# Linear attention's last two heads spread over the values' products, with operands, weight pages and weight sums at other places

## The chip, the cores and the metric

The kernel runs on one core of a Trainium2 chip. The metric is the device time of one execution in microseconds. The kernel before takes 2302.86 us, the median of three runs (2300.2, 2302.86 and 2305.18).

## The reference

One layer of a streaming encoder, 512 frames of width 2048, all in float32. A normalised input goes through one projection whose columns feed banded softmax attention (16 heads of 64), and gated linear attention (4 heads, keys of 128, values of 256). Both results go through `w_out`, then a gated feed-forward block with a short convolution, then an embedding gate, then a last normalisation.

```python
h = rms_norm(x, norm_mix_w[i])
proj = h @ w_in[i]
q_a, k_a, v_a, q_g, k_g, v_g, r_g, gate_lr = split_cols(proj, IN_SPLITS)
y_a = chunked_band_attention(q_a, k_a, v_a, att_rel_bias[i])
o_g = gated_linear_attention(q_g, k_g, v_g, log_a)
y_g = rms_norm(o_g, gla_norm_w[i]) * jax.nn.silu(r_g)
x = x + concat([y_a, y_g]) @ w_out[i]
h = rms_norm(x, norm_ffn_w[i])
u = causal_depthwise_conv(h @ w_ffn_up[i], w_ffn_conv[i], b_ffn_conv[i])
x = x + (gelu(u_gate) * u_val) @ w_ffn_down[i]
h = rms_norm(x, norm_ple_w[i])
x = x + sigmoid(h @ w_ple_gate[i]) * (p[i] @ w_ple_proj[i])
return rms_norm(x, final_norm_w)
```

## The kernel before

Every weight travels as a **page** of 128 x 1024 float32 (512 KB). A page is loaded by a DMA that SyncE issues, ScalarE copies it to a rounded high part, VectorE subtracts to get the low part, and TensorE multiplies three times (high by high, high by low, low by high). `wtile` does this for one page. Raw pages, high parts and low parts come from three **rings** of three buffers each (`wr`, `wh`, `wl`), so the raw page n+3 can be loaded only after VectorE has split page n, and the high part n+3 can be written only after TensorE has done with page n.

Large products are done with seven block products instead of eight (`PLAIN`: P1, P2, P6, P5, P7, P3, P4). Each multiplies a block of the weights, or a sum of blocks, by a block of the activations, or a sum of blocks. The activations' seven **operands** (R11, R21, N2, N1, T3, R22, T4) lie in DRAM after the first stage; `Stage.load` brings one half of one operand back (512 KB), `Stage.split` makes its two parts. The weight sums S1 to S4 are made ahead in DRAM: `sum_begin` copies a block from DRAM to DRAM on SyncE's queue, `sum_add` adds a second block with an accumulating DMA on GpSimd's queue. A list of such steps (`sum_chores`) is worked off either by `wtile` (one step a page, from the list `chores`) or at numbered steps of the later stages (`agenda`).

The order of stages:

1. The values of linear attention, and its four heads. `gla_proj(hd)` makes the decays and the two projections `pk` and `pq`; `gla_core(hd)` is a generator in six pieces, run piece by piece: the decayed keys (`kd2`, `eb2`); the transposes `pkt`, the matrix `pat`, the copy `kT` and the masked `attnT`; the states `pu` and `S`; the outputs `po` and their squares; the norm `msw`, `rg`; the last scaling and the store to `ond`.
2. **The values' products** of softmax attention: 7 products of 4 pages, 28 pages in all, 12 matmuls a page into `va`. Pages are fetched two ahead (`value_fetch(v, n + 2)`). The last pieces of heads 2 and 3 of linear attention stand between the pages of P1 and P2 (`beside_first`, `beside_second`).
3. Two units of the embedding's product (`pp`), then the **front** stage: 8 units with the attention heads and 4 with the output gates. Then `w_out` (`wo`), the up projection (`up`), and the rest.

Each engine works in the order of its own queue. VectorE, ScalarE and TensorE instructions made while `in_order(True)` is set keep the program's order; elsewhere a list scheduler may move them. SyncE's and GpSimd's queues are also in order: a DMA that waits holds up all that stand behind it on its queue. A front unit takes raw pages from a list `free`; a page returns when it has been split (`used`), and `issue` then starts the next load that is `wanted`. A name with a star keeps one free page back for a sum that VectorE makes.

What the change touches: `wtile` (line 123), the list `free` (line 393), the sums' places in the agenda (line 960), `values_product` (line 1116), and the run of the last two heads and of the values' products (lines 1351 to 1415).

Of the kernel before, what the change touches and what calls it, by code (L numbers as in the profile page):

```python
# [8 lines left out]
F32 = mybir.dt.float32  # L9
F32R = mybir.dt.float32r  # L10
# [4 lines left out]
P = 128  # L15
# [17 lines left out]
PLAIN = ("P1", "P2", "P6", "P5", "P7", "P3", "P4")  # L33
# [9 lines left out]
def encoder_block(ctx: ExitStack, tc: tile.TileContext, A, out):  # L43
# [29 lines left out]
    def in_order(on):  # L73
        for e in (vec, act, ten):
            e.on = on
# [20 lines left out]
    def use_rings(new):  # L96
        rings.update(new)
        for ring in new:
            counts[ring] = 0
# [18 lines left out]
    def psum_aux(name):  # L118
        return aux[0](name)

    chores, hold = [], [True]

    def wtile(src, name, parts=1, between=None):
        n = src.shape[1]
        raw = page("wr", name + "_r")
        hi, lo = page("wh", name + "_h", F32R), page("wl", name + "_l", F32R)
        w = n // parts
        for i in range(parts):
            if i and between is not None:
                between()  # L130
            c = slice(i * w, (i + 1) * w)
            nc.sync.dma_start(raw[:, c], src[:, c])
            act.activation(hi[:, c], raw[:, c], AF.Copy)
            vec.tensor_tensor(lo[:, c], raw[:, c], hi[:, c].bitcast(F32), ALU.subtract)
        if chores and hold[0]:
            chores.pop(0)()
        return hi, lo

    def mm3(po, whi, wlo, act, start, stop):
# [136 lines left out]
    xa, xb = [], []  # L276
# [33 lines left out]
    X_TAGS = [(op, g) for op in PRODUCT_OPERANDS for g in range(2)]  # L310
# [79 lines left out]
            self.o = None  # L390
            self.banks = {}

    free = [f"r{i}" for i in (3, 4, 5)]
    wanted = []

    def raw_page(unit, name):
# [88 lines left out]
    def prep(i, own=None):  # L485
        prep_low(prep_high(i, own))
# [230 lines left out]
    ps_, early = [], []  # L717
# [187 lines left out]
    agenda = [[] for _ in range(len(steps) + 60)]  # L905
# [28 lines left out]
    def embedding_load(raw):  # L934
        nc.sync.dma_start(raw.rearrange("p (k t) -> p k t", k=2), A["p"].rearrange("k p t -> p k t"))
        return raw

    def embedding_split(raw, t):
        ps_[:] = [t.rearrange("p h (k t) -> p k h t", k=2)]
        act.activation(t[:, 0, :], raw, AF.Copy)  # L940
        vec.tensor_tensor(t[:, 1, :], raw, t[:, 0, :].bitcast(F32), ALU.subtract)

    raws = {}
# [13 lines left out]
        aux_tags[:] = ["b6", "b7"]  # L957
        banks.extend(("b4", "b5"))

    for i, f in enumerate(sum_chores(summed[:4])):  # L960
        agenda[2 + 5 * i + 3 * max(i - 10, 0)].append((0, f))
    for i, f in enumerate(sum_chores(summed[4:])):
        agenda[base[stages[4].units[2]] + 5 * i].append((0, f))
    agenda[base[front.units[7]] + 7 + 12].append((5, attention_done))
# [112 lines left out]
    def norm_root():  # L1077
        norm["w"] = rstd_begin(norm["ms"])

    value_sums = {}  # L1080

    def value_page(name, j):
        if name[0] == "S":
# [21 lines left out]
    def values_begin():  # L1105
        v = dict(ps=[psum_mm(f"va{i}") for i in range(4)], pages=[(p, j) for p in PLAIN for j in range(4)], tiles={}, have=set())
        for n in range(2):
            value_fetch(v, n)
        return v
# [3 lines left out]
            prod, j = v["pages"][n]  # L1113
            v["tiles"][n] = wtile(value_page(PRODUCTS[prod][0], j), f"wva_{prod}{j}")

    def values_product(v, prod, between=None):
        _, op, b = PRODUCTS[prod]
        acc2 = v["ps"][0:2] if b == "A" else v["ps"][2:4]
        fresh = prod in ("P1", "P2", "P5")
        for j in range(4):  # L1120
            n = 4 * PLAIN.index(prod) + j
            value_fetch(v, n + 2)
            if between is not None:
                between(j)
            hi, lo = v["tiles"].pop(n)
            for i in range(2):
                k = 2 * j + i
                x = front.x[op, k // 4]
                wh, wl = hi[:, i * T:(i + 1) * T], lo[:, i * T:(i + 1) * T]
                for t in range(2):  # L1130
                    sl = slice(k % 4 * 256 + t * P, k % 4 * 256 + t * P + P)
                    kw = {} if fresh else {"skip_group_check": True}
                    first, last = fresh and k == 0, k == 7
                    ten.matmul(acc2[t], x[:, 0, sl], wh, start=first, stop=False, **kw)
                    ten.matmul(acc2[t], x[:, 0, sl], wl, start=False, stop=False, **kw)
                    ten.matmul(acc2[t], x[:, 1, sl], wh, start=False, stop=last, **kw)

    def values_collect(v, prod):
        quarter, sign = {"P1": ("C11", 1), "P2": ("C11", 1), "P6": ("C12", 1), "P5": ("C22", -1),
                         "P7": ("C22", -1), "P3": ("C12", 1), "P4": ("C21", -1)}[prod]  # L1140
# [15 lines left out]
    with ExitStack() as mix:  # L1156
        vp = mix.enter_context(tc.tile_pool(name="v", bufs=1, side="right"))

        with ExitStack() as gctx:
            gp = gctx.enter_context(tc.tile_pool(name="gla", bufs=1, side="right"))  # L1160
            reset = gp.tile([P, T], F32, name="reset")
            nc.gpsimd.memset(reset, 1.0)
# [16 lines left out]
                store_pair(h1d, k, xslot(k, ""), xslot(k + 8, ""), gp.tile([P, 1024], F32, tag="tp", name="tp", bufs=2))  # L1179

            for c in range(2):
                hold[0] = c == 0
                vproj(A["w_v_g"], c, lambda t: V[:, t, c * T:(c + 1) * T], c == 0, input_pair if c else None)
            hold[0] = True

            upr = page("wr", "up_r")[:, :T]
            nc.gpsimd.memset(upr[96:P], 0.0)
# [163 lines left out]
            cores = [gla_core(2, *st)]  # L1351
            step = lambda n: next(cores[n], None)

            def middle():
                in_order(True)
                for n in range(2):
                    step(0)
                in_order(False)

            nxt = gla_proj(3, middle)  # L1360
            cores.append(gla_core(3, *nxt))
            hctx.close()
            xb.append(ctx.enter_context(tc.tile_pool(name="xb", bufs=1, reuse_waits="tile")))
            pad = xb[0].tile([P, 8], F32, tag="pad", name="pad")
            nc.gpsimd.memset(pad, 0.0)
            for op, g in X_TAGS[:8]:
                front.load(op, g)
            in_order(True)
            va = values_begin()
            for g in range(2):  # L1370
                front.split("R11", g)
            step(0)
            nxt[-1]()

            def beside_first(j):
                if j:
                    step(0)
                if j > 1:
                    front.split("R21", j - 2)
                    step(1)  # L1380

            def beside_second(j):
                step(1)
                if j % 2:
                    front.split("N2", j // 2)

            values_product(va, "P1", beside_first)
            values_collect(va, "P1")
            values_product(va, "P2", beside_second)
            values_collect(va, "P2")  # L1390

    xa.append(ctx.enter_context(tc.tile_pool(name="xa", bufs=1, side="right", reuse_waits="tile")))
    for op, g in X_TAGS[8:]:
        front.load(op, g)

    ectx = ExitStack()
    early.append(ectx.enter_context(tc.tile_pool(name="early", bufs=1, side="right", reuse_waits="tile")))
    raws["p"] = embedding_load(early[0].tile([P, 1024], F32, tag="pT", name="pT"))

    values_product(va, "P6", lambda j: front.split("N1", j // 2) if j % 2 else None)  # L1400
    values_collect(va, "P6")
    values_product(va, "P5", lambda j: front.split("T3", j // 2) if j % 2 else None)
    values_collect(va, "P5")
    values_product(va, "P7", lambda j: front.split("R22", j // 2) if j % 2 else None)
    embedding_split(raws["p"], early[0].tile([P, 2, 1024], F32R, tag="ps", name="ps"))
    values_collect(va, "P7")
    issue()
    values_product(va, "P3", lambda j: front.split("T4", j // 2) if j % 2 else None)
    values_collect(va, "P3")
    values_product(va, "P4")  # L1410
    free.extend(("r0", "r1", "r2"))
    issue()
    prep(0)
    prep(1)
    values_collect(va, "P4")
# [276 lines left out]
```

## Time and profile before

| what | us |
|---|---|
| median of three runs | 2302.86 |
| the profiled execution, its own time | 2303.16 |
| its span, first to last instruction | 2300.8 |
| VectorE busy | 1878.6 |
| ScalarE busy | 1312.1 |
| GpSimd busy | 183.8 |

The span is 2.4 us shorter than the time of the same execution. TensorE's granted clock is 0.99 of full speed over the whole span. A busy time is a sum over one engine. An idle time in square brackets in a timeline row is the idle time of that engine just before the instruction, with what ended it. A DMA share is the mean busy share of the core's 16 DMA engines in a stretch.

### The profile page before, as it was taken

Reading aid. Unit: us, or ns where it says so; the run is one execution under the profiler, and the core shown is the slowest. Engines: PE = TensorE matmul, PEld = TensorE weight load, DVE = VectorE, ACT = ScalarE, POOL = GpSimd, SP = SyncE. Lnnn points to the kernel's source line nnn. Section 1 sums busy time; section 2 is a strip of 40 time slices with the busy share of each in tenths; the row PEclk is TensorE's granted clock in tenths of the full one; section 3 lists DMA queues with packets and bytes.
Section 4 is the critical chain, followed back from the end, with each engine's and each line's share of the span. In section 5 each row is a group of like instructions: output and inputs, shape, how many; then the busy total and the mean of one; then the engine's idle time right before and its main releaser. Section 6 shows DMA issues by size and latency. Waiting matters only on the chain.

```text
span 2300.8 us, 45116 instructions
## 1 busy us (share of the span) xinstructions
PE 2252.0 (98%) x17960; PEld 2180.4 (95%) x17960; DVE 1878.6 (82%) x2580; ACT 1312.1 (57%) x1925; POOL 183.8 (8%) x225
## 2 busy tenths in 40 slices
PE   9998799999989999999999999999999999999997
PEld 7787679999989999999999999999999999999997
DVE  7556567988678888899888888888888787898987
ACT  6354456776565575555555555555564454656766
POOL 0010000110100001111111111000000000000000
PEclk9999999999999999999999999999999999999999
DMA  7985578888898898999999987777786876968896
GB/s 273 276 229 184 190 226 246 234 228 233 254 379 257 268 314 224 282 291 290 289 274 277 275 237 217 211 217 206 225 299 216 270 236 212 349 234 321 290 286 208
DMA packets 215219, 588.09 MB, mean 256 GB/s; under 512 B 23168, under 2 KB 74624, under 8 KB 215008
## 3 DMA queue, kind: packets, MB, share of 16 engines
q1 hardware_dynamic: 181568, 474.28, 57.8%
q0 software_dynamic: 29952, 107.49, 25.2%
q10 hardware_dynamic: 3488, 3.44, 0.4%
q8 instruction: 140, 2.29, 0.4%
q14 instruction: 71, 0.58, 0.1%
HBM read 506.48 MB, written 141.56 MB: 282 GB/s over the span
## 4 chain that ended last, share of the span: by engine, by line
PE 85%; DMA 5%; DVE 5%; ACT 2%; issue 1%; SPq 0%; DVEq 0%; ACTq 0%
PE accA L65 42%; PE accC L65 21%; PE accB L65 10%; PE va L65 2%; DVE wl L65 1%; PE pp L65 1%; PE psc L65 1%; DMA on<-ond 1%; DMA wv_r<-in_w_v_g 1%; PE ptr L65 1%; PE py L65 1%; PE v L264 1%; PE v L263 1%; PE v L265 1%; DMA wo_N<-mix_N 1%
## 5 line engine op out<-in xcount | busy, mean ns | idle before, releaser
L65 DVE TENSOR_TENSOR wl<-s,wh 128x1024 fp32r<-128x1024 f32 (+1 forms) x365 | 437.6, 1199 | 71.6 <-ACT wh L65 70.6
L65 ACT ACTIVATE wh<-l 128x1024 fp32r<-128x1024 f32 (+1 forms) x308 | 319.1, 1037 | 183.3 <-PE accC L65 118.1
L65 DVE TENSOR_TENSOR wl<-l,wh 128x1024 fp32r<-128x1024 f32 (+1 forms) x308 | 367.6, 1193 | 57.2 <-ACT wh L65 56.8
L65 ACT ACTIVATE wh<-s 128x1024 fp32r<-128x1024 f32 (+1 forms) x365 | 378.1, 1036 | 35.4 <-DVE s L65 21.0
L65 ACT ACTIVATE u<-accA 128x256 f32<-128x256 f32 x290 | 109.7, 378 | 366.2 <-PE accA L65 365.9
L65 DVE TENSOR_TENSOR s<-s,l 128x1024 f32<-128x1024 f32 (+1 forms) x168 | 201.4, 1199 | 9.9 <-DMA s<-in_w_blk 9.2
L65 PE MATMUL accA<-up_T,wh 128*128 128x256 f32 x1408 | 178.8, 279 | 0.0
L65 PEld LDWEIGHTS accA<-up_T,wh 128*128 128x128 f32 x1408 | 170.3, 188 | 0.0
L65 DVE SCALAR_TENSOR_TENSOR cv<-u,cw,cv 128x511 f32<-128x511 f32 (+1 forms) x176 | 131.6, 748 | 3.1
L426 POOL DMA_DIRECT2D s<-in_w_up x84 | 74.2, 883 | 733.0 <-DMA s<-in_w_up 366.5
L65 PE MATMUL accA<-up_T,wl 128*128 128x256 f32 x704 | 96.6, 279 | 0.0
L65 PE MATMUL accA<-dn_T,wh 128*128 128x256 f32 x704 | 90.1, 279 | 0.0
L65 PE MATMUL accA<-up_R,wh 128*128 128x256 f32 x704 | 89.8, 280 | 0.0
L65 DVE TENSOR_TENSOR u<-u,accC 128x256 f32<-128x256 f32 x98 | 40.9, 418 | 59.5 <-PE accC L65 58.3
L65 PE MATMUL accA<-up_N,wh 128*128 128x256 f32 x704 | 89.4, 279 | 0.0
L65 PE MATMUL accC<-up_N,wh 128*128 128x256 f32 x704 | 89.4, 279 | 0.0
L65 PE MATMUL accC<-up_R,wh 128*128 128x256 f32 x704 | 89.4, 279 | 0.0
L65 PE MATMUL accB<-up_R,wh 128*128 128x256 f32 x704 | 89.4, 279 | 0.0
L65 PEld LDWEIGHTS accA<-up_T,wl 128*128 128x128 f32 x704 | 88.1, 188 | 0.0
L65 ACT ACTIVATE u<-accC 128x256 f32<-128x256 f32 x94 | 36.0, 383 | 89.5 <-PE accC L65 88.8
L65 PEld LDWEIGHTS accA<-dn_T,wh 128*128 128x128 f32 x704 | 85.7, 188 | 0.0
L65 PEld LDWEIGHTS accA<-up_R,wh 128*128 128x128 f32 x704 | 85.2, 188 | 0.5 <-issue 0.5
(426 smaller groups left out, 5257.4 us busy)
## 6 DMA issues: line engine op xcount, KB each, us to landing
l<-in_w_up SPq DMA_DIRECT2D x132, 512.0 KB, 6.6
s<-in_w_up SPq DMA_DIRECT2D x84, 512.0 KB, 6.1
s<-in_w_up POOLq DMA_DIRECT2D x84, 512.0 KB, 7.6
l<-in_w_dn SPq DMA_DIRECT2D x56, 448.0 KB, 4.9
l<-in_w_blk SPq DMA_DIRECT2D x36, 512.0 KB, 5.7
l<-in_w_out SPq DMA_DIRECT2D x28, 512.0 KB, 5.5
l<-in_w_dn SPq DMA_DIRECT2D x28, 512.0 KB, 5.4
s<-in_w_blk SPq DMA_DIRECT2D x24, 512.0 KB, 5.2
```

Of the source, the lines that this page charges most:

```text
L65: ins = f(*args, **kw)
L263: nc.tensor.matmul(ps[t], h1[kt][:, 0, sl], wh, start=kt == 0, stop=False)
L264: nc.tensor.matmul(ps[t], h1[kt][:, 0, sl], wl, start=False, stop=False)
L265: nc.tensor.matmul(ps[t], h1[kt][:, 1, sl], wh, start=False, stop=kt == KD - 1)
L426: nc.gpsimd.dma_start(t, src("L22" if name == "S1" else "L11"), accum_op=ALU.add)
```

## The change

- `wtile` works off as many steps of `chores` as `hold[0]` says, instead of one or none.
- The sums of the first two `wo` units (4 copies and 4 adds each) leave the agenda of the front stage. They are put on `chores` ahead of head 3's projections, with two steps a page there and one a page afterwards. The sums of the first two `up` units stay in the agenda, now at steps 2, 9, 16 and so on to 65 instead of 42 to 108.
- The first piece of head 2's core is issued ahead of `gla_proj(3)`, and only the second piece in its middle.
- Head 3's pieces and head 2's last ones are set to fixed pages of the values' products by a table `plan`; head 3 stands one page further from head 2.
- The operands are loaded in the program two halves of an operand at a time, at set pages, instead of eight halves ahead of P1 and six behind P2. The splits are set to pages as well.
- The raw ring has six pages from the values' products on (r3, r4, r5, r2, r0, r1 instead of three). So r3 to r5 are no longer free for the front stage's first loads; all six come free at page 25, with `issue`.

```diff
-    chores, hold = [], [True]
+    chores, hold = [], [1]
...
-        if chores and hold[0]:
-            chores.pop(0)()
+        for _ in range(hold[0]):
+            if chores:
+                chores.pop(0)()
...
-    free = [f"r{i}" for i in (3, 4, 5)]
+    free = []
...
-    for i, f in enumerate(sum_chores(summed[:4])):
-        agenda[2 + 5 * i + 3 * max(i - 10, 0)].append((0, f))
+    for i, f in enumerate(sum_chores(summed[2:4])):
+        agenda[2 + 7 * i].append((0, f))
...
             value_fetch(v, n + 2)
-            if between is not None:
-                between(j)
+            for f in plan.get(n, ()):
+                f()
...
-            def middle():
+            def pinned(f):
                 in_order(True)
-                for n in range(2):
-                    step(0)
+                f()
                 in_order(False)
 
-            nxt = gla_proj(3, middle)
+            pinned(lambda: step(0))
+            chores.extend(sum_chores(summed[:2]))
+            hold[0] = 2
+            nxt = gla_proj(3, lambda: pinned(lambda: step(0)))
+            hold[0] = 1
...
-            for op, g in X_TAGS[:8]:
-                front.load(op, g)
-            in_order(True)
-            va = values_begin()
-            for g in range(2):
-                front.split("R11", g)
-            step(0)
-            nxt[-1]()
...
-            def beside_first(j):
-                if j:
-                    step(0)
-                if j > 1:
-                    front.split("R21", j - 2)
-                    step(1)
-
-            def beside_second(j):
-                step(1)
-                if j % 2:
-                    front.split("N2", j // 2)
...
-    for op, g in X_TAGS[8:]:
-        front.load(op, g)
...
-    values_product(va, "P4")
-    free.extend(("r0", "r1", "r2"))
-    issue()
...
+    for page_, k in ((1, 0), (3, 0), (4, 0), (2, 1), (4, 1), (5, 1), (6, 1), (8, 1), (9, 1)):
+        at_page(page_, lambda k=k: step(k))
+    at_page(10, gla_done)
+    at_page(16, open_early)
+    for op, loads, splits in (("R21", (0, 1), (2, 3)), ("N2", (2, 3), (5, 7)), ("N1", (4, 5), (9, 11)), ("T3", (10, 11), (13, 15)),
+                              ("R22", (12, 13), (17, 19)), ("T4", (14, 15), (21, 23))):
+        for g in range(2):
+            at_page(loads[g], lambda op=op, g=g: front.load(op, g))
+            at_page(splits[g], lambda op=op, g=g: front.split(op, g))
+    at_page(20, lambda: embedding_split(raws["p"], early[0].tile([P, 2, 1024], F32R, tag="ps", name="ps")))
+    at_page(25, lambda: free.extend(("r0", "r1", "r3", "r4", "r5", "r2")), issue)
+
+    for g in range(2):
+        front.load("R11", g)
+    in_order(True)
+    use_rings({"wr": ("r3", "r4", "r5", "r2", "r0", "r1")})
+    va = values_begin()
+    for g in range(2):
+        front.split("R11", g)
+    nxt[-1]()
+    step(0)
+    for p in PLAIN:
+        values_product(va, p)
+        if p == "P4":
+            prep(0)
+            prep(1)
+        values_collect(va, p)
```

More of the change, by code (lines that the diff above doesn't have):

```diff
@@ L1078, in norm_root @@
         norm["w"] = rstd_begin(norm["ms"])
-    value_sums = {}
+    value_sums, plan = {}, {}
     def value_page(name, j):
@@ L1114, in value_fetch, with values_product @@
             v["tiles"][n] = wtile(value_page(PRODUCTS[prod][0], j), f"wva_{prod}{j}")
-    def values_product(v, prod, between=None):
+    def values_product(v, prod):
         _, op, b = PRODUCTS[prod]
@@ L1155, in encoder_block @@
     nc.gpsimd.memset(shim, 0.0)
-    with ExitStack() as mix:
+    if True:
+        mix, gctx = ExitStack(), ExitStack()
         vp = mix.enter_context(tc.tile_pool(name="v", bufs=1, side="right"))
-        with ExitStack() as gctx:
+        if True:
             gp = gctx.enter_context(tc.tile_pool(name="gla", bufs=1, side="right"))
@@ L1181, in encoder_block @@
             for c in range(2):
-                hold[0] = c == 0
+                hold[0] = int(c == 0)
                 vproj(A["w_v_g"], c, lambda t: V[:, t, c * T:(c + 1) * T], c == 0, input_pair if c else None)
-            hold[0] = True
+            hold[0] = 1
             upr = page("wr", "up_r")[:, :T]
@@ L1352, in encoder_block @@
             step = lambda n: next(cores[n], None)
-            def middle():
+            def pinned(f):
                 in_order(True)
-                for n in range(2):
-                    step(0)
+                f()
                 in_order(False)
-            nxt = gla_proj(3, middle)
+            pinned(lambda: step(0))
+            chores.extend(sum_chores(summed[:2]))
+            hold[0] = 2
+            nxt = gla_proj(3, lambda: pinned(lambda: step(0)))
+            hold[0] = 1
             cores.append(gla_core(3, *nxt))
@@ L1387, in encoder_block @@
[L1387 to L1392, printed above, removed]
-    for op, g in X_TAGS[8:]:
-        front.load(op, g)
-    ectx = ExitStack()
-    early.append(ectx.enter_context(tc.tile_pool(name="early", bufs=1, side="right", reuse_waits="tile")))
-    raws["p"] = embedding_load(early[0].tile([P, 1024], F32, tag="pT", name="pT"))
@@ L1400, in encoder_block @@
[L1400 to L1406, printed above, removed]
-    issue()
-    values_product(va, "P3", lambda j: front.split("T4", j // 2) if j % 2 else None)
@@ L1409, in encoder_block, with gla_done, open_early @@
-    values_collect(va, "P3")
-    values_product(va, "P4")
-    free.extend(("r0", "r1", "r2"))
[L1412 to L1415, printed above, removed]
+    def gla_done():
+        gctx.close()
+        mix.close()
+        xa.append(ctx.enter_context(tc.tile_pool(name="xa", bufs=1, side="right", reuse_waits="tile")))
+    ectx = ExitStack()
+    def open_early():
+        early.append(ectx.enter_context(tc.tile_pool(name="early", bufs=1, side="right", reuse_waits="tile")))
+        raws["p"] = embedding_load(early[0].tile([P, 1024], F32, tag="pT", name="pT"))
@@ new lines, in at_page @@
+    def at_page(n, *fs):
+        plan.setdefault(n, []).extend(fs)
+    for page_, k in ((1, 0), (3, 0), (4, 0), (2, 1), (4, 1), (5, 1), (6, 1), (8, 1), (9, 1)):
[7 more added lines that the diff above has]
+            at_page(splits[g], lambda op=op, g=g: front.split(op, g))
```

## The prediction

> **What bounds the kernel now.** I began with the page's busy times, and then cut the span into its stages.
>
> ```profile
> span 2300.8 us, 45116 instructions
> PE 2252.0 (98%) x17960; PEld 2180.4 (95%) x17960; DVE 1878.6 (82%) x2580; ACT 1312.1 (57%) x1925; POOL 183.8 (8%) x225
> ```
>
> TensorE is busy for 98% of the span, so the whole kernel has 48.8 us of idle TensorE time to give, plus what its matmuls lose after a stall. The table by stretch (busy time of PE, PEld, DVE, ACT, POOL, then granted clock, DMA share, GB/s) says where.
>
> ```profile
> core 0: us, PE busy (x) PEld busy (x) DVE busy (x) ACT busy (x) POOL busy (x), PEclk, DMA share, GB/s
> 155.00:175.70 20.70, 20.64 (x105) 16.91 (x104) 13.25 (x25) 14.66 (x19) 0.00 (x0) 1.00 0.30 80
> 175.70:199.00 23.30, 23.30 (x127) 19.69 (x128) 13.90 (x21) 11.33 (x15) 0.00 (x0) 1.00 0.39 137
> 199.00:221.00 22.00, 16.34 (x76) 13.18 (x74) 11.87 (x19) 6.93 (x10) 0.10 (x1) 0.92 0.47 167
> 221.00:289.00 68.00, 52.73 (x243) 41.96 (x243) 41.47 (x52) 31.45 (x37) 0.00 (x0) 0.89 0.58 208
> 345.00:600.00 255.00, 255.00 (x2270) 248.68 (x2269) 217.56 (x510) 173.73 (x342) 27.95 (x32) 1.00 0.85 232
> 600.00:684.00 84.00, 74.07 (x546) 71.26 (x545) 60.88 (x83) 50.02 (x77) 7.31 (x9) 0.94 1.02 346
> 684.00:2230.00 1546.00, 1544.48 (x13212) 1542.70 (x13211) 1334.14 (x1603) 876.24 (x1218) 126.50 (x145) 1.00 0.86 262
> 2230.00:2301.00 71.00, 59.07 (x498) 57.98 (x497) 55.95 (x92) 41.75 (x73) 3.46 (x4) 0.93 0.68 215
> ```
>
> TensorE waits in three places: 5.7 us at 199 to 221 and 15.3 us at 221 to 289 (head 3's projections and the values' products), 9.9 us at 600 to 684 (end of the front stage, start of `wo`, with the DMA engines full), and 11.9 us at the end. The front stage and all from 684 to 2230 are dense. The change touches nothing at the end. In the timeline of TensorE the waits have names:
>
> ```profile
> 208.45 0.63 PE L65 MATMUL pkt<-ident,kd 128*128 128x128 f32 x4 [4.63 <-DVE kd L65]
> 221.28 0.50 PE L65 MATMUL va<-wva_P_h,in_R 128*128 128x512 f32 x1 [1.31 <-ACT in_R L65]
> 242.05 1.11 PE L65 MATMUL pkt<-ident,kd 128*128 128x128 f32 x4 [4.79 <-DVE kd L65]
> 273.20 0.50 PE L65 MATMUL va<-wva_P_l,in_N 128*128 128x512 f32 x1 [1.30 <-DVE wva_P_l L65]
> 288.88 0.80 PE L65 MATMUL va<-wva_P_h,in_N 128*128 128x512 f32 x1 [7.25 <-ACT wva_P_h L65]
> 616.64 2.08 PE L65 MATMUL accC<-in_N,wl 128*128 128x256 f32 x8 [3.65 <-DVE wl L65]
> 642.10 1.79 PE L65 MATMUL accC<-in_N,wl 128*128 128x256 f32 x8 [3.02 <-DVE wl L65]
> 681.76 2.14 PE L65 MATMUL accA<-wo_N,wh 128*128 128x256 f32 x16 [3.25 <-ACT wh L65]
> ```
>
> **Part one, the first transposes (208.45).** Head 2's `kd` stands on VectorE behind head 3's `kf`, `en` and `dd`. In the built order of the changed kernel it stands right behind head 1's two scalings, which end at 203.4:
>
> ```profile
> 202.00 1.41 DVE L65 SCALAR_TENSOR_TENSOR pair_r<-pair_r,cols,rg 128x512 f32<-128x512 f32 x2
> 207.62 0.68 DVE L65 TENSOR_TENSOR kd<-dd,dec 128x512 f32<-128x512 f32 x1
> ```
>
> So `kd` is ready 4.3 us earlier. But `pkt` has moved too: in the new order only one matmul of `pq` stands ahead of it, where 19 of them did before (19 x 0.237 = 4.5 us, by the 71 matmuls of `va`, the same shape, in the last row of part two). TensorE idles from about 199.4 to 204.2 instead of 203.6 to 208.4, and `pq` ends near 218.6 as now. Worth: 0, bounds -0.5 to +0.5.
>
> **Part two, the operands.** SyncE's rows show what holds them now:
>
> ```profile
> 206.52 9.18 SPq L132 DMA_DIRECT2D wva_P_r<-in_w_v_a  x2
> 215.76 1.86 SPq L353 DMA_DIRECT2D in_R<-h_R  x4
> 272.45 1.15 SPq L353 DMA_DIRECT2D in_T<-h_T  x2
> 277.30 31.45 SPq L132 DMA_DIRECT2D wva_P_r<-va_S  x11
> ```
>
> The program of the change spreads the loads over pages, but in the built order of SyncE's queue the first eight operand halves still stand in one row, and the six later ones too. Before the first eight there now stand all eight pages of P1 and P2. The last of these reuses page 1's buffer and so waits for page 1's split, which waits for `pq`; the same split gates the first operand now. R11 is then issued at about 215.5, as now, and the stall at 221 stays. Worth: 0.
>
> What changes is behind it. Page 9's load stood behind six operand halves and `pT` (issue 277.30) and landed 10.4 us later, which is the 7.25 us stall:
>
> ```profile
> 277.30 10.37 DMA wva_P_r<-va_S
> 290.14 18.71 PE va L65 x71
> 317.56 16.83 PE va L65 x71
> ```
>
> With six raw pages the pages up to P7's second are issued ahead of that row of six (the built order says so), and the third, issued near 271 behind six loads of 1.5 us each (part four) and so landed by some 283, is not multiplied before 286. So this stall goes, and with it what follows it: 1.0 us between the one matmul at 288.88 and the next at 290.14, and the slow matmuls after that, 18.71 against 16.83 us for 71. Sum 7.25 + 1.0 + 1.88 = 10.1 us.
>
> **Part three, head 3 a page further.** At 242.05 TensorE waits for head 3's `kd`, which stands on VectorE behind head 2's norm. In the new order one more page (12 x 0.237 = 2.8 us by the last row above) stands ahead of `msw` and another ahead of `pkt`, and `kd` stands ahead of the norm's chain. I went through the three queues in their new order by hand, with 1.06 us on ScalarE and 1.2 us on VectorE for a split:
>
> ```profile
> L65 DVE TENSOR_TENSOR wva_P_l<-wva_P_r,wva_P_h 128x1024 fp32r<-128x1024 f32 x15 | 18.2, 1223 | 22.4 <-ACT wva_P_h L65 22.3
> L65 ACT ACTIVATE wva_P_h<-wva_P_r 128x1024 fp32r<-128x1024 f32 x14 | 14.6, 1058 | 14.1 <-PE va L65 7.3 <-DVE pair_r L65 3.4 <-DMA wva_P_r<-in_w_v_a 2.2
> ```
>
> By this, `kd` is ready at 236.0, TensorE comes to `pkt` at 238.8. The wait of 4.79 us goes, and also its slow clock, 2.75 against 1.50 us for the sixteen products of `pat`, and by the same ratio 0.5 us for `pkt`:
>
> ```profile
> 181.38 1.50 PE pat L65 x16
> 243.16 2.75 PE pat L65 x16
> ```
>
> The wait for a low part at 273.20 (1.30 us) goes as well, since each split is then two pages ahead; so does about 0.9 of the 1.6 us of smaller waits at 221 to 289 (15.3 - 0.3 - 4.8 - 1.3 - 7.3). In their place come: `pu` behind `kT`, which now stands on ScalarE behind the eviction of P1 and a split, 1.1 us; the outputs `po` of both heads, 0.3 and 0.6 us behind the states on VectorE; the first page of P5, 0.3 us. Sum 4.79 + 1.25 + 0.5 + 1.3 + 0.9 - 2.3 = 6.4 us. Bounds: 0, if other waits on those two crowded queues take its place, and 8.7 without new ones.
>
> **Part four, the `wo` sums.** Eight copies and eight adds move to between 155 and 235. Their price comes from the queues' totals:
>
> ```profile
> q1 hardware_dynamic: 181568, 474.28, 57.8%
> q0 software_dynamic: 29952, 107.49, 25.2%
> ```
>
> 57.8% of 2300.8 us over 474.28 MB is 2.8 us a MB, 1.5 us for a page on SyncE's queue; the same for GpSimd's queue gives 5.4 us a MB, 2.8 us an add. Eight of each are 8 x 1.5 + 8 x 2.8 = 34 us of full DMA time (46 if a copy counts its reading and its writing). Between 155 and 221 the DMA engines are idle for 66 - 6.2 - 9.1 - 10.3 = 40 us. It fits, barely. But the second unit's four adds stand on GpSimd behind a memset that waits for `pq`'s first matmuls, now at about 208, so two or three of them meet R11's loads. I charge 2 us, bounds 0 and 5.7 (two adds whole, ahead of R11). What waits for R11: the whole chain of pages.
>
> By the Trainium skill ("DMA: Bandwidth & Descriptors", Queues, rings and completion order) each DMA engine takes turns between the queues that have work, packet by packet, so an add would hold R11 back by its own length, 2.8 us, and no more; the sum would be 0.8 us worse. No run here shows two queues meeting at that place.
>
> **Part five, the end of the front stage.** What these moves and the new steps take away there is traffic of the `up` sums, in the stretch with a DMA share of 1.02. The rows are of SyncE's and GpSimd's timelines and of the chain of waits:
>
> ```profile
> 586.57 0.50 SPq L434 DMA_DIRECT2D up_S<-in_w_up  x1
> 592.78 1.19 POOL L438 DMA_DIRECT2D up_S<-up_S  x1
> 666.74 1.20 POOL L438 DMA_DIRECT2D up_S<-up_S  x1
> 592.28 13.29 DMA on<-ond
> 665.50 14.01 DMA wo_N<-mix_N
> ```
>
> Between 586 and 684 SyncE issues three such copies and GpSimd five adds (first and last are shown), 3 x 1.5 + 5 x 2.8 = 18.5 us of DMA time, and they are finished by then in the new order. The load of `on` (13.29 us for one page) shares the engines with one copy and one add, 4.3 us; the stall of 3.65 us hangs on it. I expect 7 us of the 9.9, bounds 0 (the stretch stays full with operands and weights) and 13 (all three waits and about 1 us of slow matmuls behind each, as in parts two and three).
>
> **Part six, the pages handed over.** The first front loads now wait for page 22's split and later ones, from about 16 us before the values' end, where three were long there:
>
> ```profile
> l<-in_w_blk SPq DMA_DIRECT2D x36, 512.0 KB, 5.7
> ```
>
> A page takes 5.7 us to land and is needed 4 to 20 us after that; the first S1 needs its load and an add, and comes about 7 us after the values' end, 10 us ahead of its product. Price 0; if it were late, every unit behind would be.
>
> **Sum.** 10.1 + 6.4 - 2 + 7 = 21.5 us. The profiled execution took 2303.16 us, 2.4 us more than its span and 0.3 above the median, so I take the sum off the median: 2302.9 - 21.5 = 2281.4, say 2281.
>
> **The rivals.**
> (a) The values' part comes as said, the later stalls stay because the loads of operands and weights alone fill that stretch: 14.5 us, 2288. For it: the share of 1.02 with only 18.5 of 98 us from the sums.
> (b) The split queues stay the limit: VectorE is busy for 41.5 of 68 us at 221 to 289 and waits in between on ScalarE, so new waits eat part three and half of part two; 5 us are left there and 5 later: 2293.
> (c) All goes: nothing meets R11, no new waits, 13 us later: 10.1 + 8.7 + 13 = 31.8, 2271.
> (d) Slower: the front stage is starved. Its pages begin later, the `up` sums fall into its dense stretch (share 0.85 with no stall), and each unit inherits the lateness of the one before. Twelve units from 345 to 600; from 1.8 us a unit the 21 us are eaten. At 2.3 us a unit: 2302.9 - 21.5 + 27.6 = 2309. Against it: eight `up` sums replace eight `wo` sums and the first third of the `up` sums, so the traffic there falls.
> (e) The change does not do what it says: the operands still stand in two rows of eight and six. This is in the sum already; if the six pages did not run ahead either, only parts three and four would be left, 4.4 us, 2298.5.
>
> **How the numbers follow.** The forecast has 0.5, (a) 0.18, (b) 0.1, (c) 0.1, (d) 0.08, (e) 0.04. Range: (c) and (b) with their own spread, 2269 to 2297. A measurement here tells 0.2%, 4.6 us, from no change, so faster means below 2298.3: forecast, (a), (b) and (c) together 0.88; (e) is the border, 0.04; (d) 0.08.
>
> **What would show it.** Part one: one wait of 4.6 to 4.8 us before `pkt`, now near 204. Part two: no wait over 1 us of TensorE between P6 and P4. Part three: the second `pkt` without a wait, `pu` with one of about 1 us. Part four: R11 landing after 221.5. Part five: `on` landing within 9 us, and less than 3 us idle between 580 and 665 of the new time. Wrong would make it: a stall in the front stage, or R11 later by more than 6 us.

## The result, and the profile after

The changed kernel takes 2271.78 us (median of four runs, 2268.81 to 2272.74) against 2304.02 us for the kernel before on the same chip. The ratio is 0.9861, with a 95% interval of 0.9843 to 0.9878: 32.2 us less. The forecast was 2281, the range 2269 to 2297. The profiled execution took 2271.67 us, 1.9 us more than its span.

First the table by stretch of the changed kernel, columns as in the prediction.

```profile
core 0: us, PE busy (x) PEld busy (x) DVE busy (x) ACT busy (x) POOL busy (x), PEclk, DMA share, GB/s
...
199.00:221.00 22.00, 16.95 (x73) 14.04 (x73) 9.66 (x16) 4.19 (x7) 2.57 (x4) 0.84 0.76 193
221.00:289.00 68.00, 63.86 (x303) 51.84 (x304) 52.80 (x62) 44.30 (x50) 0.81 (x1) 0.95 0.74 266
...
345.00:600.00 255.00, 255.00 (x2272) 248.76 (x2272) 224.14 (x522) 176.00 (x345) 24.40 (x28) 1.00 0.82 220
600.00:684.00 84.00, 84.00 (x675) 81.80 (x674) 69.92 (x93) 56.56 (x87) 3.87 (x5) 1.00 0.89 325
```

Where the kernel before had 5.66, 15.27 and 9.93 us of idle TensorE time (199 to 221, 221 to 289, 600 to 684), there are now 5.05, 4.14 and 0.00. Of the 4.14 us, 3.63 are the end of one wait, the 5.68 us in the third row of TensorE's timeline in the changed kernel. Every wait of over 0.3 us from the second row down to the last is in it:

```profile
178.62 0.60 PE L65 MATMUL pkt<-ident,kd 128*128 128x128 f32 x4
...
202.00 1.09 PE L65 MATMUL pkt<-ident,kd 128*128 128x128 f32 x4 [4.66 <-DVE kd L65]
...
224.63 0.79 PE L65 MATMUL va<-wva_P_h,in_R 128*128 128x512 f32 x1 [5.68 <-ACT in_R L65]
...
241.36 0.60 PE L65 MATMUL pkt<-ident,kd 128*128 128x128 f32 x4
...
246.77 1.56 PE L65 MATMUL pu<-Vg,kT 128*128 128x256 f32 x6 [0.31 <-ACT kT L65]
...
316.82 0.63 PE L65 MATMUL pp<-ps,wh 128*128 128x512 f32 x2
```

The first row is head 1's transposes, the second head 2's, the third the first product with R11, the fourth head 3's transposes, the last the embedding's product (`pp`) behind the values. Two rows of the kernel before are wanted beside them, from the same view:

```profile
180.78 0.60 PE L65 MATMUL pkt<-ident,kd 128*128 128x128 f32 x4
...
334.23 0.63 PE L65 MATMUL pp<-ps,wh 128*128 128x512 f32 x2
```

These rows cut the execution into three stretches, and every run below is read by them: from head 1's transposes to the first matmul with R11 (A), from there to `pp` (B), from `pp` to the end of the span (C). For the kernel before A is 221.28 - 180.78 = 40.50, B is 334.23 - 221.28 = 112.95 and C is 2300.8 - 334.23 = 1966.57.

| run | head 1's transposes | A | B | C | median | ratio to before, interval |
|---|---|---|---|---|---|---|
| before | 180.78 | 40.50 | 112.95 | 1966.57 | 2304.02 | |
| changed | 178.62 | 46.01 | 92.19 | 1952.98 | 2271.78 | 0.9861, 0.9843 to 0.9878 |
| e1, sums alone | 179.13 | 43.32 | 112.60 | 1951.85 | 2291.67 | 0.9960, 0.9945 to 0.9975 |
| e2, sums back | 179.14 | 40.60 | 91.60 | 1968.26 | 2283.28 | 0.9928, 0.9909 to 0.9946 |
| e3, three pages | 179.27 | 45.85 | 94.54 | 1954.74 | 2276.97 | 0.9895, 0.9879 to 0.9911 |
| e4, old places of the heads | 179.61 | 46.11 | 100.88 | 1954.40 | 2279.93 | 0.9913, 0.9898 to 0.9928 |
| e5, three pages and a row | 179.87 | 46.13 | 102.16 | 1952.94 | 2283.29 | 0.9911, 0.9893 to 0.9929 |
| e6, adds ahead | 180.44 | 41.50 | 91.60 | 1951.06 | 2269.91 | 0.9853, 0.9834 to 0.9872 |
| e7, keys early | 179.62 | 41.24 | 93.52 | 1950.82 | 2268.69 | 0.9849, 0.9831 to 0.9866 |
| e8, both | 181.22 | 37.25 | 92.70 | 1953.63 | 2266.15 | 0.9836, 0.9814 to 0.9857 |
| f1, changed again | 181.25 | 46.45 | 93.36 | 1953.34 | 2273.05 | 0.9883, 0.9865 to 0.9900 |
| f2, as e6 | 179.36 | 42.25 | 91.59 | 1951.20 | 2267.01 | 0.9859, 0.9843 to 0.9874 |
| f3, as e8 | 180.93 | 36.38 | 92.70 | 1953.89 | 2265.17 | 0.9850, 0.9834 to 0.9865 |

Two profiles of the same changed kernel (second row and f1) differ by 2.6 us at head 1's transposes and by 0.4, 1.2 and 0.4 us in A, B and C. So a difference under about 1.2 us in one cell says nothing, and the first column is not read as an effect of an edit: all runs lie between these two.

From before to changed the span is 31.0 us shorter: 2.2 in the start, -5.5 in A, 20.8 in B, 13.6 in C. The time was won in B and C and partly given back in A.

**A.** The chain of waits of the changed kernel has the load of R11 on it, 8.71 us from issue to landing:

```profile
214.78 8.71 DMA in_R<-h_R
```

GpSimd's timeline tells what R11 meets. The memset waits 16.10 us for `pq`, and the second unit's four adds stand behind it; the third is issued 0.6 us ahead of R11 and lands when the fourth is issued, at 222.88.

```profile
207.12 0.10 POOL L1370 MEMSET pad<- 128x8 f32 x1 [16.10 <-PE pq L143]
207.61 1.65 POOL L439 DMA_DIRECT2D wo_S<-in_w_out  x2 [0.39 <-issue]
214.15 0.81 POOL L439 DMA_DIRECT2D wo_S<-wo_S  x1 [4.89 <-DMA wo_S<-in_w_out]
222.88 0.81 POOL L439 DMA_DIRECT2D wo_S<-wo_S  x1 [7.92 <-DMA wo_S<-wo_S]
```

R11 lands at 223.49, so the third add is in flight nearly all that time, and the fourth for the last 0.6 us of it. R11's issue itself hangs on `pq`: it stands 2.71 us ahead of the start of `pu`, which follows `pq`'s last matmul on TensorE. The row is from TensorE's timeline of the changed kernel:

```profile
217.49 1.46 PE L65 MATMUL pu<-Vg,kT 128*128 128x256 f32 x6
```

**B.** SyncE's timeline shows the row of the six later halves still in one piece. The first page behind it is issued at 274.11, and TensorE does not wait for it:

```profile
270.27 1.13 SPq L354 DMA_DIRECT2D in_T<-h_T  x2
271.45 1.00 SPq L354 DMA_DIRECT2D in_R<-h_R  x2
272.50 1.49 SPq L354 DMA_DIRECT2D in_T<-h_T  x2
274.11 0.36 SPq L132 DMA_DIRECT2D wva_P_r<-va_S  x1
```

**C.** Two of the three waits of before hung on loads of `on`, the third on a load of `wo_N`. The second wait's row is one of VectorE's timeline of before; VectorE needs this load ahead of the low part that TensorE waits for:

```profile
638.09 1.23 DVE L65 TENSOR_TENSOR u<-u,on 128x1024 f32<-128x1024 f32 x1 [6.75 <-DMA on<-ond]
```

SyncE issues that load at 629.72, so it lands after 8.4 us: it was not slow but issued late, and what held it stays open. The first wait hung on a load that SyncE issues at 605.63, once the one before it has landed after 13.29 us, and the third on a load of `wo_N` that took 14.01. The last line in the view of the tile `on` gives its loads from issue to landing (least, median, most). The changed kernel:

```profile
DMA to landing us min/median/max: 7.0/8.2/9.6
```

And the kernel before, where the slowest took 13.3 us:

```profile
DMA to landing us min/median/max: 6.9/9.0/13.3
```

The slowest load of `wo_N` took 14.0 us before and takes 8.2 in the changed kernel (the same line of the view of `wo_N`).

### The profile page after: what moved, and what is told of

It is laid out like the page before. It is cut to its first block, busy times and chain, and to the rows that moved or that the text cites. A ratio compares the mean times of both kernels' runs of the same rounds, so it can differ in the third digit from the quotient of the medians.

```text
span 2269.8 us, 45122 instructions
## 1 busy us (share of the span) xinstructions
PE 2244.2 (99%) x17960; PEld 2175.6 (96%) x17960; DVE 1878.0 (83%) x2580; ACT 1311.7 (58%) x1925; POOL 182.8 (8%) x225
## 4 chain that ended last, share of the span: by engine, by line
PE 90%; DVE 4%; DMA 3%; ACT 2%; issue 1%; SPq 0%; DVEq 0%; ACTq 0%
PE accA L65 44%; PE accC L65 22%; PE accB L65 11%; PE va L65 3%; PE pp L65 1%; PE psc L65 1%; PE py L65 1%; DVE wl L65 1%; DMA wv_r<-in_w_v_g 1%; PE ptr L65 1%; DMA l<-in_w_ple_gate 1%; PE v L265 1%; PE v L264 1%; PE v L266 1%; PE po L65 1%
```

## The experiments

All medians and intervals are in the table above. e1 to e4 ran on one chip (before there: 2301.41), e5 to e8 on one (2304.66), f1 to f3 on one (2299.09).

**e1: the kernel before, with only the sums moved.** `wtile` has the loop of the changed kernel here, which this needs.

```diff
...
-    for i, f in enumerate(sum_chores(summed[:4])):
-        agenda[2 + 5 * i + 3 * max(i - 10, 0)].append((0, f))
+    for i, f in enumerate(sum_chores(summed[2:4])):
+        agenda[2 + 7 * i].append((0, f))
...
+            chores.extend(sum_chores(summed[:2]))
+            hold[0] = 2
             nxt = gla_proj(3, middle)
+            hold[0] = 1
```

> The kernel before with the sums alone moved: the first two wo units' sums on the list of chores ahead of head 3's projections, two steps a page there, the up units' at steps 2 to 65. Theory (the sums' traffic made the three stalls at 600 to 684): TensorE idle in that stretch falls from 9.9 us to under 2, some 13 us with the slow matmuls behind them; R11 lands some 4 us later because the adds of the second wo unit meet it; together 2302.9 - 13 + 4 = 2294, 2290 to 2298. Rival (those stalls went because the values' part ends earlier or in another rhythm): 9 to 10 us idle remain there, and R11's delay makes it 2304 to 2308.

2291.67, 9.7 us below before and inside the theory's band. In TensorE's timeline of e1 the stall at P5 stands untouched, and R11 is late:

```profile
222.45 0.50 PE L65 MATMUL va<-wva_P_h,in_R 128*128 128x512 f32 x1 [4.26 <-ACT in_R L65]
...
289.67 0.80 PE L65 MATMUL va<-wva_P_h,in_N 128*128 128x512 f32 x1 [7.29 <-ACT wva_P_h L65]
...
335.05 0.63 PE L65 MATMUL pp<-ps,wh 128*128 128x512 f32 x2
```

C is 14.7 us shorter, A 2.8 longer, B the same within 0.4. All that the sums do is in A and C: the three stalls at the end of the front stage go by the sums' move alone. The stretch from 600 to 684 in e1's table by stretch has one more thing to read (columns as before):

```profile
600.00:684.00 84.00, 84.00 (x674) 81.65 (x673) 70.96 (x93) 57.45 (x86) 3.81 (x5) 1.00 1.00 350
```

A DMA share of 1.00 and not a microsecond of idle TensorE. In the kernel before the same window had 1.02 and 9.93 us of it. (At 600 the two are at the same point within 1 us, by 684 e1 is some 14 us ahead.) So a full share alone doesn't make a wait. What the waits hung on was a load that landed too late, and in e1 the slowest load of `on` took 9.8 us (least, median, most, as above), that of `wo_N` 9.1:

```profile
DMA to landing us min/median/max: 7.4/8.1/9.8
```

Beside both slow loads of the kernel before, GpSimd issues adds of the `up` sums: one at 592.78, 0.5 us behind the load of `on` that took 13.29 us (592.28), and two at 666.15 and 666.74, behind the load of `wo_N` that took 14.01 (665.50). In e1 the last add of these sums is issued at 568.26, in the changed kernel at 549.95. So these loads may have been held as R11 is in A. e2 has an add 0.4 us behind the load of `on` at 569.78 again, and its slowest load takes 13.6 us; but it has two adds behind the last load of `wo_N` too, and there the slowest takes 10.0 and TensorE does not wait. No run parts the adds from the sums' copies.

**e2: the changed kernel, with the sums back in their old places.** It takes the two lines out that put the first two units on `chores`, and restores the agenda.

> The changed kernel with the sums at their places of before (steps 2 to 108 of the later stages, none beside head 3's projections). Theory: the stalls at the end of the front stage come back, 13 us, and R11 lands 4 us earlier: 2271.8 + 13 - 4 = 2281, 2277 to 2285. Rival: the stalls stay away, 2266 to 2270.

2283.28, 11.5 us above the changed kernel and inside the theory's band. TensorE's timeline has two waits at the front stage's end again (three before), and R11 early:

```profile
216.94 1.46 PE L65 MATMUL pu<-Vg,kT 128*128 128x256 f32 x6
219.74 0.50 PE L65 MATMUL va<-wva_P_h,in_R 128*128 128x512 f32 x1 [1.33 <-ACT in_R L65]
...
594.22 1.30 PE L65 MATMUL accC<-in_N,wl 128*128 128x256 f32 x8 [3.59 <-DVE wl L65]
...
620.10 2.08 PE L65 MATMUL accC<-in_N,wl 128*128 128x256 f32 x8 [4.46 <-DVE wl L65]
```

The chain of waits of e2 has the load of R11:

```profile
214.24 4.36 DMA in_R<-h_R
```

R11 lands in 4.36 us instead of 8.71. A is 40.60, which is what it was before (40.50): without the sums there, none of the other edits makes it longer. C is 15.3 us longer than in the changed kernel.

**e3: the changed kernel with three raw pages.**

```diff
-    free = []
+    free = [f"r{i}" for i in (3, 4, 5)]
...
-    at_page(25, lambda: free.extend(("r0", "r1", "r3", "r4", "r5", "r2")), issue)
+    at_page(20, issue)
+    at_page(25, lambda: free.extend(("r0", "r1", "r2")), issue)
...
-    use_rings({"wr": ("r3", "r4", "r5", "r2", "r0", "r1")})
```

> The changed kernel with three raw pages in the values' products, r3 to r5 free for the front stage's first loads from the start as before. Theory (part two of the prediction, 10.1 us): pages of P5 stand again behind the six operand halves, a stall of 5 to 8 us returns near 275, with its slow matmuls 8 to 10 us: 2281, 2277 to 2284. Rival (the spacing of the pages' splits, not the ring, removed it): 2270 to 2274.

2276.97, just below the theory's band and above the rival's. The ratio to before is 0.9895, against 0.9861 and 0.9883 for the changed kernel on two chips (f1 below is the second), a loss of 7.8 or 2.8 us, and the second lies within the intervals. B is 2.4 us longer than in the changed kernel's first profile and 1.2 longer than in f1. The stall at P5 does not come back. In its timeline TensorE waits 0.60 us there, and 0.57 and 0.41 at two later pages:

```profile
281.87 0.51 PE L65 MATMUL va<-wva_P_l,in_N 128*128 128x512 f32 x1 [0.60 <-DVE wva_P_l L65]
...
319.66 0.63 PE L65 MATMUL pp<-ps,wh 128*128 128x512 f32 x2
```

SyncE's timeline of e3 says why. With three pages a page's load can't run ahead, and so the halves that the program loads at set pages come to stand between the pages instead of ahead of them:

```profile
272.57 0.32 SPq L132 DMA_DIRECT2D wva_P_r<-va_S  x1
272.99 0.38 SPq L354 DMA_DIRECT2D in_R<-h_R  x1
273.70 0.35 SPq L132 DMA_DIRECT2D wva_P_r<-va_S  x1
```

So the six pages are not needed for what the prediction gave them; loads set apart do the same. Which of the two pays can't be seen with either in place, hence e5.

**e4: the changed kernel with the last pieces of the heads at their old pages.**

```diff
-    for page_, k in ((1, 0), (3, 0), (4, 0), (2, 1), (4, 1), (5, 1), (6, 1), (8, 1), (9, 1)):
+    for page_, k in ((1, 0), (2, 0), (3, 0), (2, 1), (3, 1), (4, 1), (5, 1), (6, 1), (7, 1)):
```

> The changed kernel with the pieces of heads 2 and 3 at the pages of before (head 3 one page nearer). Theory (part three, 6.4 us): the second pkt waits 4 to 5 us again for kd, near 243: 2278, 2275 to 2281. Rival (ScalarE and VectorE are the limit there whatever the place): 2270 to 2274, with the wait at another instruction.

2279.93, 8.2 us above the changed kernel and inside the theory's band. B is 8.7 us longer (7.5 against f1), and the two waits that part three spoke of are back in TensorE's timeline:

```profile
245.68 1.12 PE L65 MATMUL pkt<-ident,kd 128*128 128x128 f32 x4 [3.87 <-DVE kd L65]
...
276.34 0.50 PE L65 MATMUL va<-wva_P_l,in_N 128*128 128x512 f32 x1 [1.28 <-DVE wva_P_l L65]
...
326.60 0.63 PE L65 MATMUL pp<-ps,wh 128*128 128x512 f32 x2
```

**e5: as e3, with the six later halves and `pT` in one row at page 10.**

```diff
-    at_page(16, open_early)
-    for op, loads, splits in (..., ("T3", (10, 11), (13, 15)), ("R22", (12, 13), (17, 19)), ("T4", (14, 15), (21, 23))):
+    for op, loads, splits in (..., ("T3", (10, 10), (13, 15)), ("R22", (10, 10), (17, 19)), ("T4", (10, 10), (21, 23))):
...
+    at_page(10, open_early)
```

> The changed kernel with three raw pages again (as in the run with three pages), and with the six later operand halves and pT issued in one row at page 10, as they were before the change. Theory: the six halves in one row ahead of the pages made the stall of 7.25 us at P5; six raw pages or loads set between the pages each take it away alone, so without both it is back: a wait of 4 to 8 us ahead of a page of P5, and 6 to 10 us more than the run with three pages (2276.97): 2283 to 2287. Rival: head 3's later place alone took the stall away, since SyncE's queue is then further ahead: no wait over 1.5 us at P5, 2275 to 2279.

2283.29, 6.3 us above e3 as medians stand; but the two ran on different chips, and their ratios to before, 0.9911 and 0.9895, are 3.7 us apart with intervals that overlap. The trace decides it. TensorE's timeline of e5 has the stall back, in its second row:

```profile
226.00 0.80 PE L65 MATMUL va<-wva_P_h,in_R 128*128 128x512 f32 x1 [6.13 <-ACT in_R L65]
...
289.16 0.79 PE L65 MATMUL va<-wva_P_h,in_N 128*128 128x512 f32 x1 [5.97 <-ACT wva_P_h L65]
...
328.16 0.63 PE L65 MATMUL pp<-ps,wh 128*128 128x512 f32 x2
```

SyncE's timeline of e5, from the last two halves to the pages:

```profile
274.95 1.04 SPq L354 DMA_DIRECT2D in_T<-h_T  x2
...
276.73 23.49 SPq L132 DMA_DIRECT2D wva_P_r<-va_S  x8
```

The page stands behind six halves and `pT` again, lands 11.2 us after its issue by the chain of waits, and TensorE waits 5.97 us. B is 7.6 us longer than in e3 and 10.0 longer than in the changed kernel (8.8 against f1). Either six pages or loads set apart take the stall away; without both it stays, whatever the heads' places.

No run was made for the loads of the eight first halves. In SyncE's timeline of the changed kernel they still stand in one row, four from 214.78 and four from 217.64 on, so their new places in the program moved nothing there.

**e6 and e7: what is left in A.** e6 puts the second unit's adds ahead of the memset (`hold[0] = 3` in place of 2 for head 3's projections). e7 makes head 2's decayed keys inside head 1's core, ahead of head 1's norm:

```diff
             for hd in range(1, 3):
                 nxt = gla_proj(hd)
-                for _ in gla_core(hd - 1, *st):
-                    pass
+                for n, _ in enumerate(gla_core(hd - 1, *st)):
+                    if hd == 2 and n == 3:
+                        cores = [gla_core(2, *nxt)]
+                        pinned(lambda: step(0))
                 st = nxt
-            cores = [gla_core(2, *st)]
...
-            pinned(lambda: step(0))
```

The loop now stands behind the definition of `pinned`.

> The changed kernel with three steps of the wo sums a page instead of two, so that the second unit's four adds stand ahead of the memset on GpSimd's queue that waits for pq. Theory: these adds, issued from 207.6 on, are what holds R11 back (8.7 us from issue to landing against 4.4 before); issued ahead they meet nothing, R11 lands within 6 us of its issue, TensorE begins with R11 some 4 us earlier, and the kernel takes 2266 to 2269. Rival: the pages of P1 and P2 and the operands fill the DMA engines there anyway, or the adds only move into the pages' loads: 2271 to 2273.

> The changed kernel with head 2's decayed keys made inside head 1's core, ahead of its norm, so that kd stands ready at about 190 and the transposes ahead of pq. Theory: the wait of 4.66 us at pkt and its slow clock (about 1.9 us) go; the last page ahead of R11 on SyncE's queue waits for pq's progress, so R11 is issued earlier by about as much, but the adds on GpSimd move with it and meet R11 as now: 2265 to 2268. Rival: R11 is bound by the DMA engines and not by pq, so the time saved at pkt is waited for at R11: 2270 to 2273.

e6: 2269.91 by its median, 0.9 us short of the theory's band; its trace has all of it. TensorE's timeline of e6:

```profile
180.44 0.60 PE L65 MATMUL pkt<-ident,kd 128*128 128x128 f32 x4
...
219.18 1.46 PE L65 MATMUL pu<-Vg,kT 128*128 128x256 f32 x6
221.94 0.50 PE L65 MATMUL va<-wva_P_h,in_R 128*128 128x512 f32 x1 [1.29 <-ACT in_R L65]
```

The chain of waits of e6, its row for R11:

```profile
216.47 4.33 DMA in_R<-h_R
```

GpSimd's timeline of e6, where the last add is issued ahead of the memset:

```profile
202.62 0.81 POOL L439 DMA_DIRECT2D wo_S<-wo_S  x1 [7.08 <-DMA wo_S<-wo_S]
209.28 0.10 POOL L1370 MEMSET pad<- 128x8 f32 x1 [5.86 <-PE pq L143]
```

R11 lands in 4.33 us and A is 4.5 us shorter than in the changed kernel. e7: 2268.69. The wait at the transposes is gone, and TensorE waits longer at R11 instead, 8.37 against 5.68 us, as TensorE's timeline of e7 shows:

```profile
197.98 0.60 PE L65 MATMUL pkt<-ident,kd 128*128 128x128 f32 x4
...
220.86 0.80 PE L65 MATMUL va<-wva_P_h,in_R 128*128 128x512 f32 x1 [8.37 <-ACT in_R L65]
```

The chain of waits of e7 has the reason:

```profile
208.75 10.98 DMA in_R<-h_R
```

The adds move ahead with `pq` and meet R11 for longer than in the changed kernel: the third is issued 0.2 us ahead of it (208.55), the fourth 2.5 us ahead of its landing (217.24). Of the 6.5 us expected (4.66 and 1.9) A keeps 4.8. The time lies between the bands of theory and rival, 0.7 us from the theory's.

**e8: both.**

> Both of the two runs above: keys early, and three steps of the wo sums a page. Theory: the two savings add up, 2261 to 2265. Rival: both are bound by the same loads ahead of R11, and the two together give no more than the better one alone.

2266.15, 1.2 us above the theory's band. A is 37.25, 8.8 us shorter than in the changed kernel: the two nearly add up (4.5 and 4.8). R11 lands in 5.99 us there (6.14 in f3) and not in 4.33: the last add is issued 8.0 us ahead of it (6.0 in f3) where e6 has 13.9, so the end of that add may still meet it. e8 also has two waits of 0.69 and 1.44 us at the end of the front stage, which f3, the same kernel, does not show. Since these gains are of the size by which one kernel's median differs from chip to chip, the changed kernel and two of these were run once more side by side.

> The changed kernel once more, on the same chip as the two below. Expected 2269 to 2274, as on record.

> Three steps of the sums a page, once more. Theory, from its trace (R11 lands 4.33 us after its issue instead of 8.71, and from the first transposes of head 1 to the embedding's product it is 5.1 us shorter): 3 to 6 us below the changed kernel of this call. Rival, from its median in the first run (2269.9 against 2271.8): 0 to 3 us below.

> Both edits once more. Theory, from the traces (8.2 us shorter from the first transposes of head 1 to the embedding's product than the changed kernel, 2.1 us of new idle time at the end of the front stage): 5 to 7 us below the changed kernel of this call. Rival: as three steps of the sums alone, within 1 us of it.

2273.05, 2267.01 and 2265.17: 6.0 and 7.9 us below the changed kernel beside them. f2's theory holds; f3 gains a little more than expected. The intervals of f1 and f2 still touch (0.9865 and 0.9874), those of f1 and f3 only at 0.9865. All four times of f3 (2262.55 to 2266.98) and of f2 (up to 2268.61) lie below all four of f1 (2271.46 to 2276.26). So the version of f3 beats both kernels, its ratio to before being 0.985 (0.9834 to 0.9865). Its timeline has head 2's transposes without a wait and R11 at 217.31:

```profile
199.28 0.60 PE L65 MATMUL pkt<-ident,kd 128*128 128x128 f32 x4
...
217.31 0.50 PE L65 MATMUL va<-wva_P_h,in_R 128*128 128x512 f32 x1 [3.52 <-ACT in_R L65]
```

## Why the prediction was right, step by step

The direction was right, and each term of the sum was at the place named. Three of them were mis-sized, in both directions, and the errors did not cancel: 21.5 us forecast, 31.0 in the spans. The time lies 9.2 us below the forecast and 2.8 us above the lower end of the range, and 2.2 of the 31.0 us are at the start, within the spread of one kernel.

- **Part one, 0.** Right: e2, whose sums are in the old places, has A at 40.60 against 40.50. The wait went with `pkt` from 208.45 to 202.00 and kept its length (4.63, 4.66 us). e7 shows the cause: with `kd` made earlier the wait is gone.
- **Part two, 10.1.** Right in size: e5 against the changed kernel, 10.0 in B (8.8 against f1). What failed is the step "with six raw pages": e3 has three and almost no stall. The price belongs to two edits of which one is enough, and the prediction gave all of it to one, since its reading of SyncE's built order had only the order with six pages in it. What the six pages are worth beside the loads is 1.2 to 2.4 us in B, hardly more than the spread.
- **Part three, 6.4 of at most 8.7.** The size of one term was off: the 2.3 us of new waits at `pu`, at the outputs and at P5. `pu` waits 0.31 us and the others do not show. e4 gives 8.7, the bound without new waits. With three pages and a row it is more: e1 has B at 112.60, e5 at 102.16, 10.4 us (e1 also has the first operands at their old places). Likewise part two is worth 11.7 with the heads at their old places (e1 to e4). Either order leads from e1 to the changed kernel, 20.4 of the 20.8 us in B. That each is worth 1.7 more without the other is little above the spread of one cell, and stays open.
- **Part four, -2, bounds 0 and -5.7.** The mechanism was right, the size near the far bound: A is 5.4 us longer than in e2. R11 lands 4.35 us later (8.71 against 4.36), and is issued 1.05 us later counted from head 2's transposes (214.78 - 202.00 = 12.78 against 214.24 - 202.51 = 11.73). That the 4.35 us are the second unit's adds and not the rest of the traffic is shown by e6, where the last of them is issued 13.9 us ahead of R11 and 4.33 is back. The 1.05 us are not the adds' work: from head 2's transposes to `pu` it takes 15.49 us in the changed kernel, 15.37 in e6 (219.18 - 203.81) and 14.43 in e2 (216.94 - 202.51), and R11 is issued 2.7 us ahead of `pu` in all three. `pq` itself took longer; the sums' part in that, if any, is not shown. The prediction said that two or three adds would meet R11's loads; the third overlapped with R11 itself and the fourth with its end, and the two at 207.61 with the pages ahead of it. By the Trainium skill ("DMA: Bandwidth & Descriptors", Queues, rings and completion order) engines that take turns would let an add cost R11 its own length, 2.8 us by the queues' totals; the trace has 4.35 for one add and a little of the next, so the rule's mechanism may hold, but not the size worked out from it.
- **Part five, 7, bounds 0 and 13.** The largest error. C is 13.6 us shorter: the 9.93 us of idle time, and 3.7 us beside them, which the slow matmuls behind the waits account for: 24 matmuls take 5.29 us behind the first (616.64 to 621.93) and 4.45 behind the second (642.10 to 646.55), where the changed kernel takes 2.81 for the same ones (595.42 to 598.23), 4.1 us more in all; behind the third there is next to nothing. e1 has 14.7 and e2 gives 15.3 of it back, with nothing changed but the sums. The failing step is "I expect 7 of the 9.9, bounds 0 (the stretch stays full with operands and weights)": a full stretch was taken for a limit by itself. e1 has a share of 1.00 and no wait. What counted was when single loads came: the slowest of `on` lands after 13.3 us before and 9.6 after, that of `wo_N` after 14.0 and 8.2, and one load was issued late. The sign that the prediction set, `on` within 9 us, was too strict: 9.6 here and 11.0 in e5 made no stall.
- **Part six, 0.** Right: 345 to 600 has no idle time. Rival (d) falls with it.
- **Rivals.** (c), everything goes and nothing meets R11, has the right time by the wrong story: R11 was met, at 5.5 us, and 2.0 more in B, 0.6 more in C and 2.2 at the start made that good. (a) kept the waits of C, all of which went. (b) fell with the 0.31 us at `pu`. (e) came nearest to part two: the row of six is indeed still a row, and the pages ran ahead of it. Its own sum, 4.4 us, leaves part five out without a reason; with part five's 7 it is 11.4, 2291.5.

## What to carry to other kernels

A stretch with full DMA engines is not yet a bound: look for the loads that its waits hang on, for when they are issued and land, and for what is issued beside them. Where two edits of a change can each remove one stall, price them as one, and leave both out in an experiment before either is called the cause. Background transfers that move out of a late stretch should be issued so that nothing holds their queue up: here one memset of 0.10 us that waited 16.10 us held four of them back, until the last two met the load that mattered most.

## What the runs showed that was not expected

A plain load of 512 KB that met accumulating adds of 512 KB landed after 8.71 and 9.37 us (the changed kernel twice) and 10.98 (e7), against 4.36, 4.33 and 4.48 where they were not there or long issued (e2, e6, f2). The 4.35 us between the first of each are over one and a half times the 2.8 us that an add takes by its queue's totals. And the way up to head 1's transposes took 2.6 us more in one execution of the changed kernel than in another, more than half of what a measurement here can tell from no change.
